# w_down: one direct pair instead of two ahead of the seven-product runs, and seven pairs in their first group

## The chip, the core and the metric

The kernel is one encoder layer on one NeuronCore of a Trainium2 chip. The metric is device time in microseconds, from one launch to its end; smaller is better. The core's engines each work off a queue of their own in order: TensorE (PE, with its weight loads shown as PEld), VectorE (DVE), ScalarE (ACT), GpSimd (POOL) and SyncE (SP). SP and POOL here issue the transfers (DMAs).

## What is computed

```python
h = rmsnorm(x, ffn_norm_w)
x = x + (silu(h @ w_gate) * (h @ w_up)) @ w_down
return rmsnorm(x, final_norm_w)
```

These are the last lines of the reference; an attention part and a gated linear attention part stand ahead of them. There are 512 tokens, D = 2048 and 5632 hidden columns, all in float32. The change touches only the product with `w_down`, a (512 x 5632) by (5632 x 2048) product.

## The kernel before

Every float32 product is made of three products of split operands: each operand is written as hi + lo, and hi hi, hi lo and lo hi are summed in PSUM. A split costs a cast on ACT (hi) and a subtraction on DVE (lo = source - hi).

The 5632 hidden columns are 44 tiles of 128, or 22 pairs of tiles. The activations g = silu(gate) * up of pair q lie in DRAM as `gd[q]`, stored negated in one half. The product with `w_down` is done over pairs in two ways:

- **Direct pairs**: pairs 0 and 1 at the start, and the last two (tiles 40 to 43, `LAST`) in the tail. For each of the four blocks of 512 output columns, a job of kind "B" (`run_job`, L273) takes the weights in halves (one tile of 128 rows by 512 columns); for each half it makes 4 banks x 3 = 12 matmuls of 512 columns (L303 to L305). `st.split` (L186 to L202) loads and splits the weights, three halves ahead. `g_split` (L1420) splits the activations of a pair. At the end of a job `evac_down` (L1457) scales four banks on ACT and POOL adds them to the residual in DRAM (`xd`).
- **Seven-product pairs** (class `Down`): all others, in groups X = 2..7, Y = 8..14, Z = 15..19. A 2x2 block product is made of seven products instead of eight (Strassen's scheme in Winograd's form). `self.runs` lists (column block, pairs): X for blocks 0 to 3, but Y joins in block 3, then Y for 2, 1, 0, and so on. One run here is one pair in one column block: 7 products x 2 halves x 3 = 42 matmuls of 256 columns (L1625 to L1627). The texts call the first group of runs (block 0, pairs X) r0, and r1, r2, r3 the next; run n is the n-th of its group, from 0.

What a run needs ahead of its matmuls:

- Its **weights**: `load` (L1141), `sums` (L1157 to L1159, three DVE additions) and `split`. The split of `Blocks` (L1169, L1174) casts 768 and 1024 elements a partition on ACT and subtracts both on DVE. Where `by_dma` says so, `part` (L1515 to L1517) makes the 768 ones instead with a negated cast and an accumulating DMA that POOL issues, and DVE has the 1024 one alone (L1527, L1528).
- Its **pair's operands**, made once for all four column blocks by the generator `operands` (L1533): four DVE sums (L1556 to L1559), then four splits (ACT L1568 and L1571, DVE L1569 and L1572), in three steps: the sums; the first two splits; the last two. `make(n)` takes n steps.

The order of all this is the order in which the program issues it. `down_start` (L1434) runs within the last unit of the gate and up products and starts the first loads; `before_down(c)` runs ahead of each half of the direct jobs; `Down.run` runs, ahead of each run's products, the sums and splits of the runs to come and then some steps of `make`. Steps of the last up unit's combine (L1336 to L1357) are taken in turn as urgent work between the halves of a job. Since each engine's queue is in order, an ACT cast behind an evacuation (L1457) waits for PE to end that job.

The SBUF tiles come from two sets of slots, 62 of 512 elements ("a") and 20 of 1024 ("b"). A pair's operands hold seven "a" slots until the group's last column block has used them.

## Time and profile before

| | |
|---|---|
| time, median of 3 runs | 2186.27 us (2185.27 to 2187.46) |
| the profiled execution | 2185.2 us, its span 2183.4 us |
| PE, busy share of the span | 99% |
| DVE, ACT, POOL, busy share | 73%, 56%, 15% |
| granted PE clock, mean | 0.999 |
| PE chain's share by the matmuls of w_down's runs (L1625 to L1627) | 5% each |

A row of a timeline shows the start in us, the time from the first start to the last end of the instructions that it merges, the engine, the line, the operation with output and inputs, and their count. In brackets stands the idle time ahead of it on that engine, with what ended it. Instructions of DVE and ACT overlap a little at their ends, so what one costs its engine is the distance from its start to the next one's start. PE's durations overlap still more, so PE's rate is read from starts as well. Times count from the start of the span. A row of the table by stretches gives the length, and for each engine busy time and (x) instructions; then the granted PE clock, the share of the DMA engines and GB/s.

### The profile page before, as it was taken

Reading aid. Unit: us, or ns where it says so; the run is one execution under the profiler, and the core shown is the slowest. Engines: PE = TensorE matmul, PEld = TensorE weight load, DVE = VectorE, ACT = ScalarE, POOL = GpSimd, SP = SyncE. Lnnn points to the kernel's source line nnn. Section 1 sums busy time; section 2 is a strip of 40 time slices with the busy share of each in tenths; the row PEclk is TensorE's granted clock in tenths of the full one; section 3 lists DMA queues with packets and bytes.
Section 4 is the critical chain, followed back from the end, with each engine's and each line's share of the span. In section 5 each row is a group of like instructions: output and inputs, shape, how many; then the busy total and the mean of one; then the engine's idle time right before and its main releaser. Section 6 shows DMA issues by size and latency. Waiting matters only on the chain.

```text
span 2183.4 us, 33659 instructions
## 1 busy us (share of the span) xinstructions
PE 2170.8 (99%) x12594; PEld 1911.2 (88%) x12594; DVE 1586.0 (73%) x2757; ACT 1227.7 (56%) x2040; POOL 328.9 (15%) x363
## 2 busy tenths in 40 slices
PE   9999999999999999999999999999999999999998
PEld 7888888888888888888888888888888899999996
DVE  4366665756556546888888888888888896978987
ACT  5344444444456436666666666666666664755654
POOL 0000000000000011222222222222222221211110
PEclk9999999999999999999999999999999999999999
DMA  6525635232222633889888888888988965958783
GB/s 210 162 85 141 164 91 145 90 97 87 97 87 85 215 106 98 196 194 209 200 201 208 195 208 200 200 206 199 206 201 200 288 167 178 270 157 221 235 288 115
DMA packets 256469, 376.79 MB, mean 173 GB/s; under 512 B 18064, under 2 KB 179520, under 8 KB 256305
## 3 DMA queue, kind: packets, MB, share of 16 engines
q1 hardware_dynamic: 188768, 252.03, 36.6%
q0 software_dynamic: 66352, 121.55, 28.5%
q8 instruction: 99, 1.62, 0.3%
q10 hardware_dynamic: 1184, 1.06, 0.1%
q14 instruction: 66, 0.53, 0.1%
HBM read 246.58 MB, written 35.19 MB: 129 GB/s over the span
## 4 chain that ended last, share of the span: by engine, by line
PE 96%; DVE 2%; DMA 1%; ACT 0%; issue 0%; SPq 0%; ACTq 0%; DVEq 0%
PE pd L1302 22%; PE pd L1308 12%; PE ps L303 5%; PE ps L304 5%; PE ps L305 5%; PE ps L295 5%; PE ps L296 5%; PE ps L297 5%; PE pu L1627 5%; PE pu L1626 5%; PE pu L1625 5%; PE pe L1302 4%; PE pe L1308 2%; PE ps L529 1%; PE ps L537 1%; PE ps L538 1%
## 5 line engine op out<-in xcount | busy, mean ns | idle before, releaser
L1302 PE MATMUL pd<-a,b 128*128 128x512 f32 x2112 | 528.4, 392 | 0.8 <-DVE a L1063 0.8
L1302 PEld LDWEIGHTS pd<-a,b 128*128 128x128 f32 x2112 | 378.9, 188 | 67.0 <-DVE a L1063 1.2
L1308 PEld LDWEIGHTS pd<-a,b 128*128 128x128 f32 x2112 | 288.5, 190 | 21.6
L1308 PE MATMUL pd<-a,b 128*128 128x256 f32 x2112 | 294.9, 282 | 0.0
L1209 POOL DMA_DIRECT2D b<-b x176 | 209.8, 1248 | 521.0 <-ACT b L1208 394.1
L1626 PE MATMUL pu<-b,a 128*128 128x256 f32 x1008 | 285.4, 283 | 0.1
L1627 PE MATMUL pu<-b,a 128*128 128x256 f32 x1008 | 285.3, 283 | 0.0
L1625 PE MATMUL pu<-b,a 128*128 128x256 f32 x1008 | 285.3, 283 | 0.0
L202 DVE TENSOR_TENSOR a<-b,a 128x512 fp32r<-128x512 f32 x273 | 183.7, 686 | 131.5 <-ACT a L201 120.7
L1247 ACT CAST b<-b 128x1024 fp32r<-128x1024 f32 x176 | 185.4, 1053 | 166.3 <-DVE b L1233 138.4
L1248 DVE TENSOR_TENSOR b<-b,b 128x1024 fp32r<-128x1024 f32 x176 | 214.8, 1221 | 50.3 <-ACT b L1247 26.3
L1626 PEld LDWEIGHTS pu<-b,a 128*128 128x128 f32 x1008 | 193.5, 192 | 0.4 <-DVE b L1528 0.3
L1625 PEld LDWEIGHTS pu<-b,a 128*128 128x128 f32 x1008 | 193.5, 192 | 0.0
L1627 PEld LDWEIGHTS pu<-b,a 128*128 128x128 f32 x1008 | 193.5, 192 | 0.0
L201 ACT CAST a<-b 128x512 fp32r<-128x512 f32 x273 | 162.2, 617 | 45.0 <-PE ps L305 22.3
L1330 DVE TENSOR_TENSOR a<-pd,a 128x512 f32<-128x512 f32 x132 | 91.4, 692 | 95.8 <-ACT a L1329 95.8
L1208 ACT ACTIVATE b<-b 128x768 fp32r<-128x768 f32 x176 | 149.1, 847 | 4.7 <-PE ps L305 2.9
L1210 ACT CAST b<-b 128x768 fp32r<-128x768 f32 x176 | 145.2, 825 | 0.6 <-PE ps L305 0.6
L1329 ACT COPY a<-pd 128x512 f32<-128x512 f32 x132 | 77.5, 587 | 102.1 <-PE pd L1308 102.1
L1169 ACT CAST b<-b 128x768 fp32r<-128x768 f32 x88 | 79.0, 942 | 80.8 <-issue 68.1
L1230 DVE TENSOR_TENSOR b<-b 128x512 f32<-128x512 f32 x176 | 120.4, 684 | 0.0
L595 ACT CAST b<-ps 128x512 fp32r<-128x512 f32 x64 | 37.6, 587 | 142.9 <-PE ps L529 142.9
(284 smaller groups left out, 4472.7 us busy)
## 6 DMA issues: line engine op xcount, KB each, us to landing
b<-b POOLq DMA_DIRECT2D x204, 384.0 KB, 5.5
b<-in_w_gate_dram SPq DMA_DIRECT2D x88, 512.0 KB, 4.1
b<-in_w_up_dram SPq DMA_DIRECT2D x88, 512.0 KB, 4.3
b<-in_w_down_dram SPq DMA_DIRECT2D x88, 512.0 KB, 5.8
b<-in_w_in_dram SPq DMA_DIRECT2D x48, 512.0 KB, 4.6
b<-in_w_in_dram SPq DMA_DIRECT2D x94, 256.0 KB, 4.1
b<-in_w_out_dram SPq DMA_DIRECT2D x32, 512.0 KB, 5.2
a<-a SPq DMA_DIRECT2D x96, 128.0 KB, 2.4
```

Of the source, the lines that this page charges most:

```text
L201: act.copy(h[2].t, r)
L202: dve.tensor_tensor(h[3].t, r, h[2].f, op=OP.subtract)
L1208: act.activation(lo.t, r, AF.Copy, scale=-1.0)
L1209: pool.dma_start(out=lo.f, in_=r, accum_op=OP.add)
L1210: act.copy(hi.t, r)
L1247: act.copy(hi.t, self.S[i].t)
L1248: dve.tensor_tensor(lo.t, self.S[i].t, hi.f, op=OP.subtract)
L1302: mm(o, wh.t[:, p, k], x_.t.rearrange("p s t -> p (s t)"), start=first and p == 0, stop=False, skip_group_check=True)
L1308: mm(o[:, 256:512], wl.t[:, p, k], x_.t[:, 0], start=False, stop=last and p == 1, skip_group_check=True)
L1625: mm(o, xh[:, t], wh, start=first and not loaded and h == 0, stop=False, skip_group_check=True)
L1626: mm(o, xh[:, t], wl, start=False, stop=False, skip_group_check=True)
L1627: mm(o, xl[:, t], wh, start=False, stop=last, skip_group_check=True)
```

## The change

The groups become X = 1..7, Y = 8..14, Z = 15..19. Pair 1 moves from the direct jobs to X: each direct job has two halves instead of four, and r0 to r3 have one run more each. Operand steps are taken two at a time at some places. The weights of r0's last three runs are split by DMA.

```diff
             if q == 1:
...
-                g_load(1)
             if q == 2:
                 g_split(0)
                 st.split(down_first + 2)
+                dn.make(1)
             if q == 3:
-                dn.make(1)
+                dn.make(2)
...
             def f(i):
-                if c == 0 and i == 0:
-                    g_split(1)
-                dn.make(1)
+                dn.make(2 if c and i else 1)
+                if c == 2 and i:
+                    dn.load()
                 if c == 3:
                     dn.load()
-                    if i >= 1:
-                        dn.sums(i - 1)
-                    if i == 2:
+                    dn.sums(i)
+                    if i == 0:
                         dn.split(0)
...
-                return r == 3 or r == 6 and 3 < n < 10 or r > 6 and n in (0, 1, 4)
+                return r == 0 and n > 3 or r == 3 or r == 6 and 3 < n < 10 or r > 6 and n in (0, 1, 4)
...
-                    self.make(2 if r == 3 else (r == 6) + i % 2)
+                    self.make(2 if r == 3 or r == 0 and n < 3 else 1 if r == 0 else (r == 6) + i % 2)
...
-            j = job("B", [piece512(w_down, c * 512, k) for k in (0, 2)], list(range(4)),
+            j = job("B", [piece512(w_down, c * 512, 0)], list(range(2)),
...
-        dn = Down(list(range(2, 8)), list(range(8, 15)), list(range(15, 20)))
+        dn = Down(list(range(1, 8)), list(range(8, 15)), list(range(15, 20)))
```

In the changed file the lines behind L1441 have a number lower by one (L1556 is L1555 there, L1528 is L1527).

DVE's queue in the changed kernel, behind the last up unit's L1326, in words: the operands of pair 1; half 2 of the direct weights (0 and 1 stand ahead of all this); the first part of the combine (three additions); the sums of pair 2; half 3; the first splits of pair 2; half 4; the second part of the combine; the last splits of pair 2; the sums of pair 3; half 5; the first splits of pair 3; half 6; the last part of the combine (L1357); the last splits of pair 3; the sums of pair 4; half 7. Then come the rows below.

DVE before the change, from the last direct weights to the weights of run 0 (b_1395, b_1399, b_1400) and the sums of run 1 (b_1396). The a_13xx of L202 are direct weights, those of L1572 the operands of the fifth pair.

```order
L1157 TENSOR_TENSOR b_1395_17045<-b_1390_17008 128x512
L1158 TENSOR_TENSOR b_1395_17045<-b_1395_17045,b_1390_17008 128x256
L1159 TENSOR_TENSOR b_1395_17045<-b_1395_17045,b_1390_17008 128x256
L202 TENSOR_TENSOR a_1309_17050<-b_1388_16865,a_1308_17049 128x512
L1572 TENSOR_TENSOR a_1305_17036<-a_1297_17002,a_1304_17035 128x512
L1572 TENSOR_TENSOR a_1307_17038<-a_1298_17003,a_1306_17037 128x512
L1157 TENSOR_TENSOR b_1396_17069<-b_1391_17010 128x512
L1158 TENSOR_TENSOR b_1396_17069<-b_1396_17069,b_1391_17010 128x256
L1159 TENSOR_TENSOR b_1396_17069<-b_1396_17069,b_1391_17010 128x256
L1174 TENSOR_TENSOR b_1399_17077<-b_1390_17008,b_1397_17073 128x768
L1174 TENSOR_TENSOR b_1400_17079<-b_1395_17045,b_1398_17075 128x1024
```

Behind the change, at the same place: the last direct half, then the weights of run 0 (sums b_1389, splits b_1392 and b_1393) among the splits of the fourth pair of X and the sums of the fifth.

```order
L202 TENSOR_TENSOR a_1269_16848<-b_1377_16590,a_1268_16847 128x512
L1568 SCALAR_TENSOR_TENSOR a_1274_16879<-b_1382_16736,a_1274_16879 128x256
L1571 TENSOR_TENSOR a_1276_16881<-b_1382_16736,a_1275_16880 128x512
L1157 TENSOR_TENSOR b_1389_16892<-b_1384_16839 128x512
L1158 TENSOR_TENSOR b_1389_16892<-b_1389_16892,b_1384_16839 128x256
L1159 TENSOR_TENSOR b_1389_16892<-b_1389_16892,b_1384_16839 128x256
L1174 TENSOR_TENSOR b_1392_16900<-b_1384_16839,b_1390_16896 128x768
L1174 TENSOR_TENSOR b_1393_16902<-b_1389_16892,b_1391_16898 128x1024
L1571 TENSOR_TENSOR a_1278_16883<-a_1266_16833,a_1277_16882 128x512
L1571 TENSOR_TENSOR a_1280_16885<-a_1267_16834,a_1279_16884 128x512
L1555 TENSOR_TENSOR a_1281_16922<-b_1383_16809 128x256
L1556 TENSOR_TENSOR a_1281_16922<-b_1383_16809 128x256
```

Before, the fifth pair is done and the sums of two runs are made when run 0 is split; now the fourth pair is split around run 0's weights, and the sums of runs 1 and 2 (twice three rows) and the splits of run 1 come only behind the rows shown and two more sums of the fifth pair.

DVE before the change, within r0, between the splits of run 1 (b_1405, b_1406) and of run 2 (b_1411, b_1412):

```order
L1174 TENSOR_TENSOR b_1405_17133<-b_1391_17010,b_1403_17129 128x768
L1174 TENSOR_TENSOR b_1406_17135<-b_1396_17069,b_1404_17131 128x1024
L1157 TENSOR_TENSOR b_1408_17139<-b_1393_17014 128x512
L1158 TENSOR_TENSOR b_1408_17139<-b_1408_17139,b_1393_17014 128x256
L1159 TENSOR_TENSOR b_1408_17139<-b_1408_17139,b_1393_17014 128x256
L1174 TENSOR_TENSOR b_1411_17147<-b_1392_17012,b_1409_17143 128x768
L1174 TENSOR_TENSOR b_1412_17149<-b_1402_17101,b_1410_17145 128x1024
```

Behind the change, within r0, between the splits of run 2 (b_1407 is the second of them) and of run 3 (b_1415, b_1416); b_1388 is the sixth pair, b_1412 the sums of run 4:

```order
L1174 TENSOR_TENSOR b_1407_17046<-b_1396_16956,b_1405_17042 128x1024
L1555 TENSOR_TENSOR a_1294_17055<-b_1388_16890 128x256
L1556 TENSOR_TENSOR a_1294_17055<-b_1388_16890 128x256
L1557 TENSOR_TENSOR a_1295_17056<-b_1388_16890,a_1294_17055 128x256
L1558 TENSOR_TENSOR a_1295_17056<-a_1295_17056,b_1388_16890 128x256
L1568 SCALAR_TENSOR_TENSOR a_1296_17061<-b_1388_16890,a_1296_17061 128x256
L1571 TENSOR_TENSOR a_1298_17063<-b_1388_16890,a_1297_17062 128x512
L1157 TENSOR_TENSOR b_1412_17116<-b_1394_16904 128x512
L1158 TENSOR_TENSOR b_1412_17116<-b_1412_17116,b_1394_16904 128x256
L1159 TENSOR_TENSOR b_1412_17116<-b_1412_17116,b_1394_16904 128x256
L1174 TENSOR_TENSOR b_1415_17124<-b_1387_16845,b_1413_17120 128x768
L1174 TENSOR_TENSOR b_1416_17126<-b_1403_17036,b_1414_17122 128x1024
```

Between the splits of two runs stood the sums of one run; now two of a pair's three operand steps stand there as well. Between the splits of runs 1 and 2 stand the last two steps of the fifth pair and the sums of run 3. Behind run 3 follow: the last splits of the sixth pair, the sums of the seventh, the sums of run 5, the 1024 split of run 4; the first splits of the seventh pair, the sums of run 6, the 1024 split of run 5; the last splits of the seventh pair.

## The prediction

> **What bounds the kernel now.** I read the page first, then the stretches around the change, then TensorE's and VectorE's rows there.

> ```profile
> span 2183.4 us, 33659 instructions
> PE 2170.8 (99%) x12594; PEld 1911.2 (88%) x12594; DVE 1586.0 (73%) x2757; ACT 1227.7 (56%) x2040; POOL 328.9 (15%) x363
> PE 96%; DVE 2%; DMA 1%; ACT 0%; issue 0%; SPq 0%; ACTq 0%; DVEq 0%
> ```

> TensorE (PE) is busy for 99% of the span and makes 96% of the chain that ended last: what it waits more is lost, what it computes less is gained. The next table takes the direct block (L1751's jobs) and the first run group, r0.

> ```profile
> 1723.20:1766.70 43.50, 43.50 (x194) 36.02 (x193) 38.02 (x75) 29.87 (x55) 11.98 (x15) 1.00 0.85 224
> 1766.70:1796.90 30.20, 30.20 (x253) 30.18 (x252) 29.16 (x46) 18.07 (x27) 4.09 (x7) 1.00 0.69 185
> ```

> The columns are length, then busy time of PE, PEld, DVE, ACT, POOL. PE never pauses in 73.7 us; DVE works 38.0 + 29.2 = 67.2 of them. The cover is thin here: 6.5 us.

> ```profile
> 1743.18 2.67 ACT L1457 ACTIVATE a<-pu,small 128x512 f32<-128x512 f32 x4 [3.44 <-PE pu L305]
> ...
> 1746.39 1.29 DVE L1572 TENSOR_TENSOR a<-a,a 128x512 fp32r<-128x512 f32 x2 [2.87 <-ACT a L1571]
> ...
> 1757.32 0.69 DVE L202 TENSOR_TENSOR a<-b,a 128x512 fp32r<-128x512 f32 x1 [2.16 <-ACT a L201]
> ```

> Of that, 2.87 + 2.16 = 5.03 us are waits of DVE for casts that stand behind ACT's evacuations, which wait for PE. So the slack is the length of the direct block.

> **PE's own work.** Rows of PE: the block's first matmul, r0's first, r1's first.

> ```profile
> 1723.19 0.40 PE L303 MATMUL pu<-a,a 128*128 128x512 f32 x1
> ...
> 1766.72 0.28 PE L1625 MATMUL pu<-b,a 128*128 128x256 f32 x1
> ...
> 1796.95 0.28 PE L1625 MATMUL pu<-b,a 128*128 128x256 f32 x1
> ```

> 192 direct matmuls (4 column blocks x 4 halves x 12) take 43.53 us, 0.2267 each; r0's 252 (6 runs x 42) take 30.23, 0.1200 each, 5.04 a run. The change removes 96 of the first (21.76 us) and adds 168 of the second (20.16 us): PE has **1.60 us** less to do. [...]

> **What DVE must do, and by when.** The queue shown in the change section is walked with start-to-start times of these rows.

> ```profile
> 1723.90 0.41 DVE L1326 TENSOR_TENSOR a<-pe,a 128x256 f32<-128x256 f32 x1
> ...
> 1727.60 0.42 DVE L1336 TENSOR_TENSOR b<-a 128x256 f32<-128x256 f32 x1
> ...
> 1729.00 0.42 DVE L1569 SCALAR_TENSOR_TENSOR a<-b,a 128x256 fp32r<-128x256 f32 x1
> ...
> 1730.54 1.02 DVE L1336 TENSOR_TENSOR b<-a,a 128x256 f32<-128x256 f32 x2
> 1731.47 1.29 DVE L1572 TENSOR_TENSOR a<-a,a 128x512 fp32r<-128x512 f32 x2
> ...
> 1733.28 1.22 DVE L1357 TENSOR_TENSOR b<-b,b 128x1024 f32<-128x1024 f32 x1
> 1734.42 0.42 DVE L1556 TENSOR_TENSOR a<-b 128x256 f32<-128x256 f32 x1
> ...
> 1735.88 0.69 DVE L202 TENSOR_TENSOR a<-b,a 128x512 fp32r<-128x512 f32 x1
> 1736.48 0.42 DVE L1569 SCALAR_TENSOR_TENSOR a<-b,a 128x256 fp32r<-128x256 f32 x1
> 1736.82 0.69 DVE L1572 TENSOR_TENSOR a<-b,a 128x512 fp32r<-128x512 f32 x1
> 1737.42 0.68 DVE L202 TENSOR_TENSOR a<-b,a 128x512 fp32r<-128x512 f32 x1
> 1738.02 1.29 DVE L1572 TENSOR_TENSOR a<-a,a 128x512 fp32r<-128x512 f32 x2
> 1739.23 0.68 DVE L202 TENSOR_TENSOR a<-b,a 128x512 fp32r<-128x512 f32 x1
> ```

> A pair's operands cost Q = 1.46 (four sums, 1734.42 to 1735.88), T1 = 0.34 + 0.60 = 0.94 and T2 = 1.21 (four splits): 3.61 in all. A half of direct weights (L202) costs 0.60. The combine of the last up unit, which stays, costs 1.40 + 0.93 + 1.14 = 3.47.

> ```profile
> 1763.72 2.09 DVE L1174 TENSOR_TENSOR b<-b,b 128x768 fp32r<-128x768 f32 x2
> 1765.72 0.42 DVE L1556 TENSOR_TENSOR a<-b 128x256 f32<-128x256 f32 x1
> ...
> 1770.83 0.69 DVE L1157 TENSOR_TENSOR b<-b 128x512 f32<-128x512 f32 x1
> ...
> 1772.36 2.09 DVE L1174 TENSOR_TENSOR b<-b,b 128x768 fp32r<-128x768 f32 x2
> 1774.48 0.69 DVE L1157 TENSOR_TENSOR b<-b 128x512 f32<-128x512 f32 x1
> ...
> 1874.30 1.22 DVE L1528 TENSOR_TENSOR b<-b,b 128x1024 fp32r<-128x1024 f32 x1
> 1875.43 0.42 DVE L1569 SCALAR_TENSOR_TENSOR a<-b,a 128x256 fp32r<-128x256 f32 x1
> L1169 ACT CAST b<-b 128x1024 fp32r<-128x1024 f32 x8 | 8.4, 1050 | 0.1
> ```

> A run's weights cost S = 1.53 for the sums and 2.00 for the two splits, of which 1.13 is the 1024 one (by the row at 1874.30) and so 0.87 the 768 one; by DMA only the 1.13 is left.

> As before, DVE comes to the block's work behind L1326, at 1723.90 + 0.34 = 1724.24. PE, undisturbed, is at half k at 1723.19 + 2.72k, at run n of r0 at 1744.95 + 5.04n. It wants a lower half 0.23 (direct) or 0.12 (run) later, the lower half of the sums at its third product, 1.56 later.
> - To the last direct half: three pairs 10.83, Q of a fourth 1.46, the combine 3.47, six halves 3.60, together 19.36: 1743.60. PE wants it at 1742.46: 1.1 late already.
> - Run 0: T1, S, 0.87 = 3.34: 1746.94, wanted 1745.07: 1.9 late. The 1024 split adds 1.13 and about 0.2 for ACT, whose 1.05 us cast starts only after the sums: 1748.3.
> - Run 1: T2, Q, twice S, 0.87 = 6.60: 1754.9, wanted 1750.1: 4.8 late; then 1.13.
> - Run 2: T1, T2, S, 0.87 = 4.55: 1760.6, wanted 1755.15: 5.4; then 1.13.
> - Run 3: Q, T1, S, 0.87 = 4.80: 1766.5, wanted 1760.2: 6.3; then 1.13.
> - Run 4 (by DMA): T2, Q, S, 1.13 = 5.33: 1773.0, wanted 1766.7: 6.3.
> - Run 5: T1, S, 1.13 = 3.60: 1776.6, wanted 1771.7: 4.9. From here DVE gains.

> PE's total wait is the largest of these, 6.3, with 0.1 for handing over **6.4 us**. It is not worked off later: PE has no pause to give back. The sum is -1.60 + 6.4 = +4.8 us: the profiled execution (2185.2 us, span plus 1.8) becomes 2190.0, and the median of the runs shown, 2186.27, becomes **2191.1**.

> **The rest of the edit.** Four direct loads, one load of activations and the ten splits behind them go; four weight loads, one pair's load and three accumulating transfers in r0 come (a fourth in r3).

> ```profile
> L1209 POOL DMA_DIRECT2D b<-b x176 | 209.8, 1248 | 521.0 <-ACT b L1208 394.1
> b<-b POOLq DMA_DIRECT2D x204, 384.0 KB, 5.5
> ```

> Each transfer costs POOL 1.2 us, of which it has 30.20 - 4.09 = 26 free in r0, and lands 5.5 us after issue; ACT's negated cast for run 4 comes in its queue before the casts for run 3, by an estimate at 1758, so the transfer lands at some 1765 against 1771. I cost it at nothing; late by one landing it would be 5.5. In r1 and r2 the added run costs DVE 3.65 (1770.83 to 1774.48) against PE's 5.04. In r3 a run costs 1.53 + 1.13 + two thirds of 3.61 = 5.07 against 5.04, so 0.3 us over ten runs; its fifth split is done at 1875.5 and wanted at 1857.4 + 4 x 5.04 + 1.44 = 1879.0. Both: nothing, at most 0.3. The queue of SP passes nothing that waits longer.

> **Rivals.**
> - Pair 1 is prepared ahead of the block, in DVE's waits for the last up unit:

> ```profile
> 1716.17 1.23 DVE L1248 TENSOR_TENSOR b<-b,b 128x1024 fp32r<-128x1024 f32 x1 [2.16 <-ACT b L1247]
> ...
> 1723.29 0.69 DVE L1330 TENSOR_TENSOR a<-pd,a 128x512 f32<-128x512 f32 x1 [0.70 <-ACT a L1329]
> ```

>  These alone are 2.86 us. If pair 1's 3.61 fell there, 2.8 of wait would stay: +1.2, 2187.5, not slower. It decides at whether DVE is done with pair 1 by 1724.2. Against it: the order has pair 1 behind L1326. 0.08.
> - All of the wait is covered, as now: -1.6, 2184.7. DVE would have to find 6.4 us that the rows do not show. 0.05.
> - DVE waits for ACT as well, as it does later:

> ```profile
> DVE b L1174 <- ACT b L1169: 7.5, 7, 1.7
> ```

>  One such wait, at most 1.7, in the chain above: 2192.8. Against it: those waits stand where DVE runs ahead of PE and lacks a free slot, which it does not do here. Walked with its own rows, ACT is an estimated 1 us ahead of DVE everywhere but at run 0. 0.10.
> - PE's clock falls in the wait before run 1 (2.9 us: run 0 ends at 1746.94 + 5.04 = 1752.0, run 1's split at 1754.9). The columns are as above, the clock is third from the end.

> ```profile
> 2172.00:2176.00 4.00, 2.67 (x23) 2.46 (x21) 3.65 (x9) 2.13 (x8) 0.00 (x0) 1.00 0.00 0
> 2176.00:2180.00 4.00, 0.00 (x0) 0.00 (x0) 2.03 (x7) 1.13 (x3) 0.00 (x0) 0.62 0.33 122
> ```

>  PE is busy for 2.67 us of the first row, so it ends at 2174.7; a mean of 0.62 over the second is a fall to half at about 2177.0, 2.3 us on. A whole run at half clock, 5.04 longer, would end at 1765.0; run 3 then starts at 1770.0, 9.9 late: +8.3, 2194.6. [...] 0.07.

> **How the numbers follow.** The forecast has 0.70. 0.2% is 4.4 us, about what a measurement of this kernel can tell from no change; +4.8 is just above it, and with the shown spread (2185.27 to 2187.46) some 7 in 10 of this case are slower by more: 0.50. With ACT's wait and the clock, 0.67 slower. The rest of the forecast and the two covered cases are within it, 0.31, and 0.02 is left for faster. The range takes a total wait from 2.8 us (pair 1 done early) to 9.9 (the clock's case) and leaves out full cover: 2187.5 to 2194.6.

> **What would show it.** In the profile after, PE has waits for DVE at L303 to L305 (about 1 us together) and at the first lines of r0's runs, the longest before run 1, all before r0's fifth run, none in r1 to r3; DVE has no idle time from 1724 to 1773; the block's matmuls take 0.227 and the runs' 0.120. If PE has no such waits, the walk of DVE is wrong; if they stand with DVE idle for ACT or a DMA, its cause is.

## The result, and the profile after

The changed kernel takes 2189.91 us (median of 17 runs, 2188.68 to 2193.03), the kernel before 2185.54 (17 runs, 2183.97 to 2189.81): a ratio of 1.0020, 95% interval 1.0013 to 1.0028. The profiled execution took 2189.91 us.

From the page of the changed kernel: span, busy time, and the chain that ended last.

```profile
span 2188.1 us, 33842 instructions
PE 2171.7 (99%) x12666; PEld 1915.1 (88%) x12666; DVE 1593.9 (73%) x2771; ACT 1234.7 (56%) x2046; POOL 332.4 (15%) x367
...
PE 96%; DVE 3%; DMA 1%; ACT 0%; issue 0%; SPq 0%; DVEq 0%; ACTq 0%
```

The span is 4.7 us longer, and one share of the chain has grown by a per cent: DVE. The place shows in the stretches of the changed kernel, the direct block and r0 (columns as in the prediction):

```profile
1723.73:1746.96 23.23, 22.70 (x99) 17.79 (x97) 22.88 (x48) 18.88 (x36) 11.13 (x13) 1.00 1.06 244
1746.96:1787.39 40.43, 37.31 (x295) 36.76 (x294) 39.36 (x68) 29.38 (x44) 8.01 (x11) 0.96 0.86 221
```

Where PE was busy without a pause and DVE for 67.2 of 73.7 us, DVE is now busy for 62.2 of 63.7 and PE is the one with pauses. PE's rows in the changed kernel, the first matmul of the block, two waits in it, the first matmuls of r0's runs where PE waited, and the first of r1; in brackets the wait and what ended it:

```profile
1723.73 0.40 PE L303 MATMUL pu<-a,a 128*128 128x512 f32 x1
...
1732.60 0.50 PE L304 MATMUL pu<-a,a 128*128 128x512 f32 x1 [0.30 <-DVE a L202]
...
1744.29 0.50 PE L304 MATMUL pu<-a,a 128*128 128x512 f32 x1 [0.22 <-DVE a L202]
...
1747.62 0.39 PE L1625 MATMUL pu<-b,a 128*128 128x256 f32 x1 [0.39 <-DVE b L1174]
...
1755.67 0.58 PE L1625 MATMUL pu<-b,a 128*128 128x256 f32 x1 [2.74 <-DVE b L1174]
...
1787.39 0.28 PE L1624 MATMUL pu<-b,a 128*128 128x256 f32 x1
```

The one number that the rest goes by is **PE's loss**: from the block's first matmul to r1's first are 1787.39 - 1723.73 = 63.66 us; 96 matmuls of 0.2267 and 294 of 0.1200 take 57.04; 6.62 us are lost. In the kernel before the same stretch (192 and 252 matmuls) took 73.76, and nothing was lost.

The 4.7 us of span are made up of +0.54 ahead of the block (1723.73 against 1723.19; PE's waits for the first loads of x differ by as much, 2.1 against 1.6 us), -1.60 + 6.62 for PE's saving and its loss, and -0.86 behind r1's start (400.71 us against 386.45 with three runs more, 15.12). The first and the last of these nearly cancel, and they are no larger than what differs between the profiles of the changed kernel and its versions below, where the block begins between 1722.4 and 1724.3 and the part behind r1's start takes 400.7 to 401.6 us.

### The profile page after: what moved, and what is told of

The parts are those of the page before. It is cut to its first block, busy times and chain, and to the rows that moved or that the text cites. A ratio compares the mean times of both kernels' runs of the same rounds, so it can differ in the third digit from the quotient of the medians.

```text
span 2188.1 us, 33842 instructions
## 1 busy us (share of the span) xinstructions
PE 2171.7 (99%) x12666; PEld 1915.1 (88%) x12666; DVE 1593.9 (73%) x2771; ACT 1234.7 (56%) x2046; POOL 332.4 (15%) x367
## 4 chain that ended last, share of the span: by engine, by line
PE 96%; DVE 3%; DMA 1%; ACT 0%; issue 0%; SPq 0%; DVEq 0%; ACTq 0%
PE pd L1302 22%; PE pd L1308 11%; PE pu L1625 5%; PE pu L1626 5%; PE pu L1624 5%; PE ps L303 5%; PE ps L304 5%; PE ps L305 5%; PE ps L295 5%; PE ps L296 5%; PE ps L297 5%; PE pe L1302 4%; PE pe L1308 2%; PE ps L529 1%; PE ps L537 1%; PE ps L538 1%
## 5 line engine op out<-in xcount | busy, mean ns | idle before, releaser
L1625 PE MATMUL pu<-b,a 128*128 128x256 f32 x1064 | 302.3, 284 | 3.2 <-DVE b L1174 3.1
L1626 PE MATMUL pu<-b,a 128*128 128x256 f32 x1064 | 301.7, 284 | 0.0
L1624 PE MATMUL pu<-b,a 128*128 128x256 f32 x1064 | 301.6, 283 | 0.0
L1209 POOL DMA_DIRECT2D b<-b x176 | 209.8, 1248 | 520.9 <-ACT b L1208 393.9
L1247 ACT CAST b<-b 128x1024 fp32r<-128x1024 f32 x176 | 185.3, 1053 | 166.3 <-DVE b L1233 138.5
L202 DVE TENSOR_TENSOR a<-b,a 128x512 fp32r<-128x512 f32 x265 | 178.2, 686 | 129.5 <-ACT a L201 118.5
L1248 DVE TENSOR_TENSOR b<-b,b 128x1024 fp32r<-128x1024 f32 x176 | 214.9, 1221 | 50.2 <-ACT b L1247 26.3
L1625 PEld LDWEIGHTS pu<-b,a 128*128 128x128 f32 x1064 | 204.9, 193 | 4.0 <-DVE b L1174 3.6
L1624 PEld LDWEIGHTS pu<-b,a 128*128 128x128 f32 x1064 | 204.9, 193 | 0.0
L1626 PEld LDWEIGHTS pu<-b,a 128*128 128x128 f32 x1064 | 204.9, 193 | 0.0
L201 ACT CAST a<-b 128x512 fp32r<-128x512 f32 x265 | 157.5, 618 | 45.0 <-PE ps L305 22.3
L1330 DVE TENSOR_TENSOR a<-pd,a 128x512 f32<-128x512 f32 x132 | 91.4, 692 | 95.8 <-ACT a L1329 95.8
L1208 ACT ACTIVATE b<-b 128x768 fp32r<-128x768 f32 x176 | 149.3, 848 | 4.7 <-PE ps L305 2.9
L1329 ACT COPY a<-pd 128x512 f32<-128x512 f32 x132 | 77.6, 588 | 102.0 <-PE pd L1308 102.0
L1169 ACT CAST b<-b 128x768 fp32r<-128x768 f32 x88 | 79.3, 940 | 85.6 <-issue 64.9
## 6 DMA issues: line engine op xcount, KB each, us to landing
b<-b POOLq DMA_DIRECT2D x208, 384.0 KB, 5.6
```

The costliest lines, as they stand in the source:

```text
L201: act.copy(h[2].t, r)
L202: dve.tensor_tensor(h[3].t, r, h[2].f, op=OP.subtract)
L1208: act.activation(lo.t, r, AF.Copy, scale=-1.0)
L1209: pool.dma_start(out=lo.f, in_=r, accum_op=OP.add)
L1247: act.copy(hi.t, self.S[i].t)
L1248: dve.tensor_tensor(lo.t, self.S[i].t, hi.f, op=OP.subtract)
```

## The experiments

The theory: VectorE is behind in the direct block and the first runs of r0, and each us by which its queue is behind at its worst point is a us of PE's time. The rivals: the fall of PE's clock that the trace shows in run 1 is a cost of its own; ACT's casts or transfers are what is late; r1 to r3 or PE's own work cost more than the rows said. "Walked" below means the prediction's method, the queues of the kernel in question followed row by row with the same durations, which for the changed kernel gives 5.98 us of waits.

| kernel | median us | ratio to before, 95% | block's first, r1's first matmul | PE's loss |
|---|---|---|---|---|
| changed kernel | 2189.91 | 1.0020, 1.0013 to 1.0028 | 1723.73, 1787.39 | 6.62 |
| e1_cut | 2183.72 | 0.9992, 0.9983 to 1.0001 | 1722.38, 1779.87 | 0.45 |
| e2_warm | 2189.82 | 1.0020, 1.0011 to 1.0029 | 1722.56, 1786.23 | 6.63 |
| e3_twice_before | 2186.32 | 1.0006, 0.9997 to 1.0015 | 1722.98, 1797.92 | 1.18 |
| e4_twice_after | 2194.10 | 1.0041, 1.0028 to 1.0053 | 1724.22, 1792.26 | 11.00 |
| e5_no_dma | 2190.52 | 1.0023, 1.0014 to 1.0032 | 1724.01, 1787.88 | 6.83 |
| e6_swap | 2189.08 | 1.0017, 1.0008 to 1.0026 | 1723.18, 1786.01 | 5.79 |
| e7_late_pairs | 2189.12 | 1.0018, 1.0009 to 1.0027 | 1723.07, 1785.54 | 5.43 |
| e8_all | 2185.00 | 0.9999, 0.9990 to 1.0008 | 1724.22, 1783.39 | 2.13 |
| e9_all_no_late_dma | 2185.27 | 1.0003, 0.9994 to 1.0012 | 1723.20, 1781.66 | 1.42 |
| e10_pair1_early | 2187.53 | 1.0014, 1.0005 to 1.0022 | 1724.32, 1787.28 | 5.92 |
| e11_swap_pool_sums | 2192.44 | 1.0034, 1.0021 to 1.0046 | 1723.73, 1789.97 | 9.20 |
| e12_all_pool_sums | 2190.53 | 1.0026, 1.0017 to 1.0035 | 1722.84, 1787.34 | 7.46 |

The kernel before ran beside the experiments at medians of 2184.90 to 2185.17 us, and at 2185.54 beside the changed kernel, so medians of different rows compare to some 0.6 us at best. The loss is that of the one profiled execution (for e3 the undisturbed 73.76 is taken off), so it tells small steps apart that the intervals do not.

### e1_cut: VectorE's work taken away

```
 act.copy(hi, src)
-tt(lo, src, hf, op=OP.subtract)
+todo[i] = (src, hi, hi, hf) if q < 8 else tt(lo, src, hf, op=OP.subtract) and todo[i] or todo[i]
```

> The changed kernel, but for the seven pairs of the first group VectorE's splits of the three large operands (three of the four lower halves: f2, T1/T3, T2/T4) are left out and the upper half is used in their place, so TensorE does the same products and VectorE has 1.8 us less per pair, 12.7 us in all. Theory (VectorE is late in the direct block and in r0, and nothing else costs): TensorE has no wait there, r1 begins 57.0 us after the block's first matmul (measured for the changed kernel: 63.7), and TensorE's own -1.6 us is left: 1.6 us faster than the kernel before, a ratio of 0.9993, 6.2 us faster than the changed kernel. Rival 1 (the loss is not VectorE's, but ACT's casts, a DMA, or a slower stream of matmuls): most of the 6.6 us of waits stay, ratio 1.001 to 1.002. Rival 2 (a run's matmuls cost TensorE more than the rows said, or the added runs of r1 to r3 cost): no waits, but a ratio of 1.000 or over.

Measured: 1.4 us under the kernel before by the medians, with an interval that just takes in no change. PE's only wait from the block to r1 (line, who ends it, sum, times, longest), then three of its rows: the block's first, r0's first, r1's first.

```profile
PE pu L1625 <- DVE b L1174: 0.2, 1, 0.2
```

```profile
1722.38 0.40 PE L303 MATMUL pu<-a,a 128*128 128x512 f32 x1
...
1744.15 0.28 PE L1624 MATMUL pu<-b,a 128*128 128x256 f32 x1
...
1779.87 0.28 PE L1624 MATMUL pu<-b,a 128*128 128x256 f32 x1
```

Without 12.7 us of VectorE's work one short wait is left, and 6.17 of the 6.62 us come back. The block takes 21.77 us, as 96 x 0.2267 says. So what remains of the change when VectorE keeps up is PE's own saving, and r1 to r3 add nothing. Rivals 1 and 2 fall.

### e2_warm: the clock held up

```
+def fill(self, n, r):
+    if (r, n) == (0, 1): b, h = ps.get(), self.x[1]["B11"][0]; [mm(b.t[:, 0:256], h[:, 0:P], h, start=True, stop=True) for _ in range(22)]; put(b)
...
-self.products(i)
+self.fill(n, r); self.products(i)
```

First what the clock did in the changed kernel. Its stretches around run 1, the granted clock third from the end:

```profile
1753.00:1755.00 2.00, 0.00 (x0) 0.00 (x0) 1.93 (x5) 1.74 (x3) 0.20 (x1) 1.00 1.06 173
1755.00:1756.00 1.00, 0.33 (x1) 0.33 (x2) 1.00 (x2) 1.00 (x3) 0.00 (x0) 0.72 1.18 197
1756.00:1758.00 2.00, 2.00 (x11) 2.00 (x11) 2.00 (x4) 2.00 (x4) 0.00 (x0) 0.50 1.03 198
1758.00:1760.00 2.00, 2.00 (x15) 2.00 (x15) 1.93 (x5) 2.00 (x4) 0.86 (x1) 0.78 0.88 293
```

A mean of 0.72 over 1755 to 1756 is a fall to half at 1755.4, and the matmuls stand 0.214 us apart until 1758.8, then 0.120: 3.4 us at half clock. From the row at 1755.67 to run 2's first matmul at 1762.08 are 6.41 us for 41 matmuls, 4.92 at full clock: 1.5 us of PE's time.

> The changed kernel with 22 matmuls that nothing reads (128x256, 0.12 us each, 2.64 us) put on TensorE ahead of run 1 of r0, where it waited 2.9 us and its granted clock then fell to 0.50 for some 3 us, which cost about 1.6 us. Theory (the clock's loss is hidden behind VectorE: run 3's weights are ready no sooner): the clock stays at 1.00, run 1 ends 1.6 us sooner, TensorE waits for VectorE ahead of runs 2 and 3 instead (0.6 and 0.9 us), and r1 begins at the same time after the block's start, 63.7 us within 0.3: ratio 1.002 as for the changed kernel. Rival (the clock's fall is a cost of its own): r1 begins 1.6 us sooner, at 62.1, and the time is 1.6 us less, ratio about 1.0013. If the matmuls come too late or run too long: run 1 starts later than 2.9 us behind run 0's end.

Rows of PE in e2_warm: the added matmuls, the waits ahead of runs 2 and 3, and r1's first; then the clock in the stretch where it had fallen.

```profile
1751.48 2.80 PE L1482 MATMUL pu<-a 128*128 128x256 f32 x22
...
1760.16 0.38 PE L1625 MATMUL pu<-b,a 128*128 128x256 f32 x1 [0.37 <-DVE b L1174]
...
1766.09 0.39 PE L1625 MATMUL pu<-b,a 128*128 128x256 f32 x1 [0.64 <-DVE b L1174]
...
1786.23 0.28 PE L1624 MATMUL pu<-b,a 128*128 128x256 f32 x1
```

```profile
1756.00:1758.00 2.00, 2.00 (x19) 2.00 (x18) 2.00 (x4) 2.00 (x3) 0.28 (x1) 1.00 0.93 224
```

The clock stays at 1.00, run 1 is done sooner, and PE gets the time back as waits ahead of runs 2 and 3, where the changed kernel had none: the loss is 6.63 in place of 6.62. The half clock cost nothing here; the rival falls.

### e3_twice_before and e4_twice_after: VectorE's work added

```
-dve.tensor_tensor(h[3].t, r, h[2].f, op=OP.subtract)
+for _ in range(2 if 4 <= self.n_conv - state.get("df", 1 << 20) < 12 else 1): dve.tensor_tensor(h[3].t, r, h[2].f, op=OP.subtract)
...
-down_first = len(st.halves)
+down_first = state["df"] = len(st.halves)
```

In e4 the numbers are 2 and 8 in place of 4 and 12.

> The kernel before, with VectorE's split of eight of the sixteen direct halves (the fifth to the twelfth) done twice: 8 x 0.60 = 4.8 us more for VectorE in the direct block, nothing else. Theory (the kernel before has some 5 us of cover there, VectorE's two waits for ACT of 2.87 and 2.16 us): nearly all of it is hidden, 0 to 0.5 us slower, ratio 1.0000 to 1.0003, and the two waits shrink. Rival (the kernel before has no more cover than the changed one, and the 6.6 us come from the new order): 3 to 4.8 us slower, ratio 1.0015 to 1.002.

> The changed kernel, with VectorE's split of the third to the eighth of its eight direct halves done twice: 6 x 0.60 = 3.6 us more for VectorE. Theory (VectorE is the bound from the block to r0's fifth run, so each us of its work is a us of time): 3.6 us slower than the changed kernel, r1 67.2 us after the block's first matmul, ratio to the kernel before 1.0036 to 1.004. With the half clock in it this could be up to 1 us more, since a second fall of the clock may come. Rival (the waits come from ACT, DMA or the clock): less than 1 us slower, ratio 1.002 to 1.0025.

A row of PE and one of DVE in e3; two rows of PE in e4; and two of DVE in e4, the first of them a split done twice:

```profile
1737.87 0.50 PE L304 MATMUL pu<-a,a 128*128 128x512 f32 x1 [0.83 <-DVE a L202]
...
1758.30 0.69 DVE L202 TENSOR_TENSOR a<-b,a 128x512 fp32r<-128x512 f32 x1 [0.48 <-ACT a L201]
```

```profile
1749.14 0.50 PE L304 MATMUL pu<-a,a 128*128 128x512 f32 x1 [1.63 <-DVE a L202]
...
1760.52 0.39 PE L1625 MATMUL pu<-b,a 128*128 128x256 f32 x1 [2.73 <-DVE b L1174]
```

```profile
1733.06 1.41 DVE L202 TENSOR_TENSOR a<-b,a 128x512 fp32r<-128x512 f32 x2
1734.39 0.42 DVE L1568 SCALAR_TENSOR_TENSOR a<-b,a 128x256 fp32r<-128x256 f32 x1
```

A split done twice costs VectorE 1734.39 - 1733.06 = 1.33 us where one costs 0.60: 0.73 more, not the 0.60 that the expectations took. The second one writes what the first one wrote and starts 0.72 us behind it (1.41 for both, 0.69 for one), not 0.60. So e3 adds 8 x 0.73 = 5.8 us and e4 6 x 0.73 = 4.4.

In the kernel before, these 5.8 us cost 1.18 us, at one place where the queue is short of slack for a moment; that is more than the 0 to 0.5 expected. DVE's two waits of 2.87 and 2.16 us took up the rest: one is gone and one is 0.48, 4.55 us less. In the changed kernel 4.4 us more cost 4.38 (4.2 by the medians), one for one. So there was cover, and there is none now. The clock stayed at 1.00 in e4, through the same wait of 2.7 us ahead of run 1.

A wait of PE costs it more than its bracket says. The one of 0.30 costs 0.57 in all: 1732.60 comes 0.47 us later than a matmul behind the last one would, and the next another 0.10. So handing over from VectorE takes some 0.25 us.

### e5_no_dma, e6_swap, e7_late_pairs: the order of VectorE's work

```
e5 -return r == 0 and n > 3 or r == 3 or r == 6 and 3 < n < 10 or r > 6 and n in (0, 1, 4)
e5 +return r == 3 or r == 6 and 3 < n < 10 or r > 6 and n in (0, 1, 4)
e6 -if r > 6 and n == 0:
e6 +if r > 6 and n == 0 or r == 0:
e7 -dn.make(2 if c and i else 1)
e7 +dn.make(2 if c == 2 and i else 1)
e7 -self.make(2 if r == 3 or r == 0 and n < 3 else 1 if r == 0 else (r == 6) + i % 2)
e7 +self.make(2 if r == 3 else (2, 2, 2, 3, 2, 1, 1)[n] if r == 0 else (r == 6) + i % 2)
```

> The changed kernel without the new clause of by_dma: the splits of 768 columns of r0's fifth, sixth and seventh run go back from the accumulating transfers to VectorE, 3 x 0.87 = 2.6 us more for it. Theory, walked row by row through the queues that this kernel has: these splits come behind the point where VectorE's lateness is largest, and in this form the sums of the run after next no longer stand ahead of run 4's split; TensorE's waits are 5.8 us against 6.0 walked for the changed kernel (6.5 measured): the same time within 0.5 us, ratio 1.002. The longest wait stays ahead of run 1; waits of some 0.5 and 0.2 us come ahead of run 5 and in run 6. Rival (VectorE's total work in r0 sets the time, whatever its place): 2.6 us slower than the changed kernel, ratio 1.0032.

> The changed kernel with one step turned round in r0: the splits of the next run's weights come ahead of the sums of the run after it, no work is added or taken away. Theory: at each run's first matmul VectorE then has one step of sums less (1.53 us) ahead of what TensorE wants: walked, TensorE waits 4.65 us in place of 5.98, so 1.3 us faster than the changed kernel, ratio 1.0014; the wait ahead of run 1 is 1.35 us in place of 2.9. Rival (the same work in another order takes the same time): ratio 1.002. Rival (the wait ahead of run 1 is the loss by itself, 2.9 with the half clock's 1.6): 3 us faster, ratio 1.0006.

> The changed kernel with another pace for the pairs' operands: three pairs are made ahead of r0 instead of four, the others come two to three steps a run in r0, as late as each run allows. The amount of work is the same. Theory: VectorE is 3.6 us less behind at the first runs, and the lateness is taken over by run 5, behind which all seven pairs have to be done: walked, waits of 4.5 us in place of 6.0, 1.5 us faster than the changed kernel, ratio 1.0013, with short waits ahead of runs 0 to 3 and one of 0.9 us ahead of run 5. Rival (order does not matter): ratio 1.002. Rival (four pairs ahead are what costs): all of 3.6 us gone, ratio 1.0003.

PE's waits from the block to the end of r0, as line waited for, sum, times and longest: e6, then e7.

```profile
PE pu L1625 <- DVE b L1174: 3.2, 4, 1.2
PE pu L304 <- DVE a L202: 0.5, 2, 0.3
```

```profile
PE pu L1625 <- DVE b L1174: 2.6, 4, 1.0
PE pu L1625 <- DVE b L1527: 0.9, 1, 0.9
PE pu L304 <- DVE a L202: 0.3, 1, 0.3
```

e5: 2.6 us of work behind the worst point changed the loss by 0.2 (the clock fell to 0.50 in it as in the changed kernel); total work is not what counts, its place is. e6: the loss is 0.83 less, the wait ahead of run 1 1.2 in place of 2.7; e7: 1.19 less, with the new wait ahead of run 5 (L1527) where it was expected. Both gain less than walked (1.3 and 1.5), and VectorE's own queue shows why: in e6 it pauses 0.24 us for ACT's cast at run 1 as well as at run 0, and where an operation has to wait for the one directly ahead of it, it starts 0.12 us later than the walk had it (three times up to run 4 in e6, twice up to run 5 in e7). Handing over does not add up from wait to wait, since in these profiles a late PE does not hold up VectorE; it counts once, at the last wait. There VectorE, against the instant at which an undisturbed PE would want its work, is 6.40 us late in the changed kernel (run 3), 10.77 in e4 (run 3), 5.56 in e6 (run 4) and 5.19 in e7 (run 5), against losses of 6.62, 11.00, 5.79 and 5.43. By the medians both are about 0.8 us faster than the changed kernel (0.4 when each is set against the kernel before that ran beside it), which the intervals do not tell from nothing; the traces do, since the waits stand at the places that the order gives them. Neither rival fits: not no gain, not 3 us and more.

### e10_pair1_early: the first rival of the prediction

```
 if q == 0:
-    g_load(0)
+    g_load(0); dn.make(1)
 if q == 1:
...
-    st.load()
+    st.load(); dn.make(1)
 if q == 2:
...
-    dn.make(1)
+    dn.make(2)
 if q == 3:
-    dn.make(2)
+    pass
...
-dn.make(2 if c and i else 1)
+dn.make(2 if c and i else 1 if c or i else 0)
```

> The changed kernel with one change: pair 1's operands (3.61 us of VectorE) are made in the last up unit, where VectorE waits for ACT (2.16 + 0.69 + 0.72 + 0.70 us), instead of behind L1326. Theory: VectorE comes to the direct block as before and has one pair less in it, at most 3.6 us less of wait; walked with ACT's queue (VectorE now waits 1.6 us for a cast that stands behind ACT's evacuations) 4.15 us of wait are left of 5.98, ahead of runs 1 to 3: 1.8 us faster than the changed kernel, ratio 1.0012, no wait in the direct block. Rival (all of the 3.6 us come off): ratio 1.0004. Rival (the pair holds up the up unit's last evacuations and with them the block): ratio 1.002 or over.

Stretches of e10, the granted clock third from the end:

```profile
1754.00:1758.00 4.00, 3.61 (x17) 3.61 (x18) 4.00 (x7) 4.00 (x7) 0.39 (x1) 0.50 0.97 212
1758.00:1760.00 2.00, 2.00 (x11) 2.00 (x11) 1.93 (x5) 0.87 (x3) 0.47 (x1) 0.50 1.01 348
```

No wait is left in the block, as walked, and one of 2.7 us ahead of run 1. The profiled execution was the slowest of the 11 (2190.05 us). In it the clock then stayed at 0.50 until 1760.5, twice as long as in the changed kernel, and some 28 matmuls at 0.214 us lost about 2.7 us, of which DVE's lateness behind run 1, 1.5 us walked, could hide only a part. VectorE was 4.5 us late at run 3 (ready at 1765.84, wanted at 1761.32), with handing over 4.8, and this one profile lost 5.92 us. So here the half clock did cost something of its own: about 1.2 us. The median is 2.4 us under the changed kernel, or 1.7 when each is set against the kernel before beside it; 1.8 were walked.

### e8_all, e9_all_no_late_dma: all of it together

The changed kernel with e6's line, e10's edits of down_start, and the following; e9 leaves by_dma as it was.

```
-return r == 0 and n > 3 or r == 3 or r == 6 and 3 < n < 10 or r > 6 and n in (0, 1, 4)
+return r == 0 and n > 2 or r == 3 or r == 6 and 3 < n < 10 or r > 6 and n in (0, 1, 4)
...
-dn.make(2 if c and i else 1)
+dn.make(1)
...
-self.make(2 if r == 3 or r == 0 and n < 3 else 1 if r == 0 else (r == 6) + i % 2)
+self.make(2 if r == 3 else (2, 2, 2, 2, 2, 2, 1)[n] if r == 0 else (r == 6) + i % 2)
```

> The changed kernel with four changes of VectorE's queue: the splits ahead of the sums as in e6_swap; the pairs' operands later, one step a half and two a run in r0; pair 1's operands three steps sooner, in the last up unit, where VectorE waits for ACT; and the split of 768 columns of r0's fourth run by transfer as well (0.87 us less). Theory (lateness is a sum over the queue, and each of these takes a piece of it): walked, no wait of TensorE is left, and its own 1.6 us are gained: 1.6 us faster than the kernel before, ratio 0.9993, 6 us faster than the changed kernel; with a handover or two 0.9993 to 0.9996. Rival (pair 1's steps hold up the last up unit, or a transfer or load comes late, so that new waits of 2 us or more stand in the old ones' place): ratio 1.0003 or over.

> e8_all without its fourth change: the split of 768 columns of r0's fourth run stays on VectorE (0.87 us). In e8_all the transfer for it landed some 12 us after its issue and TensorE waited 1.6 us for it ahead of run 3. Theory: that wait goes, walked 0.3 us of wait is left ahead of run 3, so 1.3 us faster than e8_all and 1.3 to 1.6 us faster than the kernel before: ratio 0.9993 to 0.9995, the sum of TensorE's gaps from the block to r1 0.3 to 0.7 us. Rival (the transfers for the fifth to seventh run are now late as well, or another wait comes in its place): ratio 0.9998 to 1.0005.

In e8, DVE where it had waited 2.16 us for ACT, the transfer for run 3 (POOL's issue), and PE where it needs it; below it, PE's waits in e9.

```profile
1717.20 1.23 DVE L1248 TENSOR_TENSOR b<-b,b 128x1024 fp32r<-128x1024 f32 x1 [0.69 <-ACT b L1247]
...
1751.06 0.86 POOL L1515 DMA_DIRECT2D b<-b  x1 [0.65 <-ACT b L1514]
...
1763.26 0.39 PE L1625 MATMUL pu<-b,a 128*128 128x256 f32 x1 [1.44 <-DMA b<-b]
```

```profile
PE pu L1625 <- DVE b L1174: 0.7, 2, 0.5
```

In e8 VectorE hardly makes PE wait any more, but the transfer took 12 us from its issue to PE's go, and its wait came in the old one's place: the rival's mechanism, at 1.6 us, though the ratio of 0.9999 lies between what the theory and the rival had. e9 takes that away. Its loss is 1.42 us, not the 0.3 to 0.7 expected, and it is not faster than the kernel before, as it should have been by 1.3 us or more: VectorE is still 1.2 us late at run 5 (ready at 1772.91, wanted at 1771.72) where 0.3 us at run 3 was walked, and handing over adds 0.25. Among what the walk lacked are the same small delays as in e6: pauses of 0.25 and 0.17 us for ACT's casts at runs 0 and 1, and 0.12 us behind each of four splits. The loss is nearly PE's whole saving. By the medians e8 and e9 do not differ. The order of VectorE's work gives back 5.2 of the 6.6 us in the profiles; no version here is measurably faster than the kernel before.

### e11_swap_pool_sums, e12_all_pool_sums: VectorE's work moved to GpSimd

```
-tt = dve.tensor_tensor
+tt, ts = dve.tensor_tensor, pool.tensor_tensor
...
-tt(t13.t[:, a], n1[:, z], n1[:, a], op=OP.subtract)
+(ts if 3 < q < 8 else tt)(t13.t[:, a], n1[:, z], n1[:, a], op=OP.subtract)
```

The other three sums are changed alike; e12 has `2 < q < 8`. e11 has e6's line, e12 all of e9 but `dn.make(2 if c == 2 and i else 1)` and `(2, 2, 2, 2, 2, 1, 1)[n]`.

> e6_swap, with the four sums of the operands of pairs 4 to 7 moved from VectorE to GpSimd: 4 x 1.46 = 5.8 us less for VectorE from the end of the direct block on. Theory (VectorE's work is the bound): if one such sum takes GpSimd 0.8 us, walked, 0.8 us of TensorE's wait is left of 4.65, 5.1 us faster than the changed kernel, ratio 0.9997, with waits only in the direct block (0.4) and one before run 2. If it takes 1.5 us, VectorE waits for GpSimd and ACT for both, and 4.2 us are left: ratio 1.001. Rival (GpSimd's sums make VectorE's own operations longer): VectorE's 512-column split takes more than 0.69 us while they run, and the ratio is 1.0015 or over.

> e9_all_no_late_dma, with the sums of the operands of pairs 3 to 7 on GpSimd (7.3 us less for VectorE) and the pairs' pace one step further ahead. Theory: with 0.8 us a sum on GpSimd no wait of TensorE is left, walked, ratio 0.9992 (1.6 us faster than the kernel before, 6 us faster than the changed one); with 1.5 us 3.2 us of wait, ratio 1.0007. Rival (the waits that were left in e9 come from handing over and from the casts' queue, not from VectorE): the same as e9, ratio 1.0000 to 1.0003.

The sums of a run's weights on VectorE between 1740 and 1785 us (busy time, mean ns of one) and its splits: in e6, then in e11.

```profile
L1157 DVE TENSOR_TENSOR b<-b 128x512 f32<-128x512 f32 x9 | 6.2, 690 | 0.2
L1174 DVE TENSOR_TENSOR b<-b,b 128x1024 fp32r<-128x1024 f32 x5 | 6.1, 1222 | 0.5 <-ACT b L1169 0.5
```

```profile
L1157 DVE TENSOR_TENSOR b<-b 128x512 f32<-128x512 f32 x8 | 8.5, 1064 | 0.2
L1174 DVE TENSOR_TENSOR b<-b,b 128x1024 fp32r<-128x1024 f32 x4 | 8.0, 2006 | 0.0
```

One row of e11:

```profile
1769.77 2.73 DVE L1157 TENSOR_TENSOR b<-b 128x512 f32<-128x512 f32 x1
```

Both are slower than what they start from, by 3.4 us (e11 against e6) and 5.3 (e12 against e9). The same instruction of VectorE takes 1064 ns in place of 690 in the mean, and its 1024-column split 2006 in place of 1222. The means mix instructions as long as before with much longer ones: the sum in the row took 2.73 us, four times its usual time, while GpSimd was at its sums (1769.51 to 1773.1), and the two splits at 1760.56 took 4.17 us in place of 2.09, while GpSimd was at its sums from 1761.20 on. VectorE had no wait for GpSimd in this stretch. So it is e11's rival: GpSimd's sums are paid for by VectorE, and VectorE's lateness is all of the loss in e11 (8.95 us in run 4, with handing over 9.20). What makes VectorE's instructions longer beside GpSimd's is in no profile.

The clock fell in both as well, for 3.4 us. That was hidden: in e12 too the loss of 7.46 us is VectorE's lateness, 7.17 us at run 3, and handing over.

## Why the prediction was right, point by point

- **PE's own saving, 1.60 us.** Right: e1's block took 21.77 us against 21.76 by the first rate, and its last five runs, which have no wait, 25.20 (1754.67 to 1779.87), 5.04 each as by the second.
- **The walk of VectorE.** Right to 0.2 us all along. Rows of DVE in the changed kernel, the last direct half and the first split of runs 0 to 5:

```profile
1743.55 0.69 DVE L202 TENSOR_TENSOR a<-b,a 128x512 fp32r<-128x512 f32 x1
...
1746.62 0.95 DVE L1174 TENSOR_TENSOR b<-b,b 128x768 fp32r<-128x768 f32 x1
1747.81 1.23 DVE L1174 TENSOR_TENSOR b<-b,b 128x1024 fp32r<-128x1024 f32 x1 [0.24 <-ACT b L1169]
...
1754.67 2.09 DVE L1174 TENSOR_TENSOR b<-b,b 128x768 fp32r<-128x768 f32 x2
...
1760.34 2.08 DVE L1174 TENSOR_TENSOR b<-b,b 128x768 fp32r<-128x768 f32 x2
...
1766.26 2.09 DVE L1174 TENSOR_TENSOR b<-b,b 128x768 fp32r<-128x768 f32 x2
...
1772.46 1.22 DVE L1527 TENSOR_TENSOR b<-b,b 128x1024 fp32r<-128x1024 f32 x1
...
1776.18 1.22 DVE L1527 TENSOR_TENSOR b<-b,b 128x1024 fp32r<-128x1024 f32 x1
```

 With 0.60, 0.87 and 1.13 from these starts the work is ready at 1744.15, 1747.49, 1755.54, 1761.21, 1767.13, 1773.59 and 1777.31. The prediction's instants, with the 0.54 us by which the block began later, are 1744.14, 1747.48, 1755.4, 1761.1, 1767.0, 1773.5 and 1777.1. DVE's only pause over 0.1 us is the 0.24 us for ACT's cast that the walk had at 0.2; the rival of a longer wait for ACT did not come.
- **PE's total wait, 6.4 us.** Measured 6.62, so the size held: VectorE is 6.40 us late at run 3 (ready at 1767.13, wanted at 1760.73) where 6.3 was forecast, and handing over, which the prediction put at 0.1 with no row for it, is some 0.25 us at the last wait. The make-up was not as told: the waits ahead of run 2 and nearly all of that ahead of run 3 are not in the profile, because run 1 at half clock used them up.
- **The clock's fall** was a rival with 0.07 and a price of +8.3. It happened in the profiled execution and cost nothing. What failed is its price: a whole run at half clock was the author's estimate, and it was 3.4 us and 1.5 us of PE's time. It came with a bracket of 2.7 us ahead of run 1, and in e12 with one of 1.9.
- **Net +4.8, 2191.1 us.** Measured 2189.91, 4.4 over the kernel before beside it. In the profile the change's own part is -1.60 + 6.62 = +5.0, and the rest, -0.3, lies ahead of the block and behind r1's start.
- **The rest of the edit at nothing.** Right: no wait from r1 to r3, and the new transfers of r0 are waited for by nobody. A landing 5.5 us behind the issue was too narrow a price for one that is late: e8's took 12 us.
- **Pair 1 ahead of the block** (2187.5 as a rival): the program that does it, e10, has a median of 2187.53, but the match is luck. The rival took all 3.61 us off the wait; in e10 DVE waits 1.40 us for one of ACT's casts in the block, by the walk 4.2 of the 6.0 us stayed, and against the kernel before beside it e10 is at +2.6, not +1.2.

## What to carry to other kernels

When a bound engine gives up work, look at the engine that feeds it: 1.6 us of TensorE's work were saved here, and with them went the 21.8 us in which VectorE could work ahead. The loss is not the feeder's total work but its worst lateness along its queue, so it can be worked out by following the queue, in order, against the instants at which the other engine wants each piece, and it is cut by moving work behind that point (e6, e7) or into earlier pauses (e10). Such a loss also hides others: here a fall of the clock cost nothing as long as the feeder was the later one (6.62 us of loss with it, 6.63 without in e2), and began to cost when the feeder was relieved (some 1.2 us in e10).

## What the runs showed of the hardware

- In the trace of the changed kernel PE's clock is 1.00 or 0.50. It changes at 7.83, 11.24, 1755.45, 1758.86 and 2182.12 us, and the times between are 1, 511, 1 and 124 times 3.4133 us. In r0 it fell to 0.50 in five of the profiles: for 3.41 us in the changed kernel, for 3.4 us in e5 (1755.90 to 1759.30), e11 and e12, and for 6.8 us, twice as long, in e10 (1753.70 to 1760.52). Stretches cut along such steps: the one ahead of the fall in the changed kernel, the one ahead of the fall in e12, and the two in e4 over which its wait of 2.7 us lies.

```profile
1752.04:1755.45 3.41, 0.90 (x8) 0.69 (x6) 3.27 (x7) 2.19 (x4) 1.16 (x2) 1.00 1.07 178
```

```profile
1750.65:1754.07 3.42, 1.52 (x13) 1.31 (x12) 3.29 (x3) 2.80 (x5) 3.42 (x5) 1.00 1.05 241
```

```profile
1755.86:1759.27 3.41, 1.93 (x17) 1.73 (x15) 3.24 (x8) 2.01 (x4) 2.18 (x3) 1.00 1.06 149
1759.27:1762.69 3.42, 2.17 (x18) 2.17 (x19) 3.42 (x6) 3.42 (x7) 0.00 (x0) 1.00 1.06 191
```
